# Rotary tables at double width, a gate row that starts later, and the low parts of queries, keys and input forms on another engine

## The chip, the cores and the metric

The kernel runs on one core of a Trainium2 chip. The core has TensorE (matrix products, written PE in a profile), VectorE (DVE), ScalarE (ACT), GpSimd (POOL) and SyncE (SP, which here only issues DMAs); each works through a queue of its own in order, and semaphores tie them together. The metric is the device time of one execution in microseconds, lower is better. Before the change it is 2218.59 us, the median of three runs (2226.13, 2218.59, 2211.78).

## The reference

Two layers of a decoder trunk on a sequence of 1024 with 1024 features, then an RMSNorm. Each layer has four mLSTM heads and four retention heads of width 256 side by side. Cut to what matters:

```python
for l in range(DEPTH):
    shift, scale, gate = split(silu(c) @ w_ada[l] + b_ada[l], 3)
    h = rmsnorm(x, norm_g[l]) * (1 + scale) + shift
    mq, mk, mv, mo, mz, mi, mf, rq, rk, rv, rz = split_cols(h @ w_in[l])
    q, k = split(silu(causal_dwconv([mq, mk], conv_w[l], conv_b[l])), 2)
    y_m = sigmoid(mo) * head_layernorm(mlstm_chunkwise(q, k, mv, mi, mf)) * silu(mz)
    rq, rk = rotary(rq, positions), rotary(rk, positions)
    y_r = head_layernorm(retention_chunkwise(rq, rk, rv)) * silu(rz)
    x = x + gate * ([y_m, y_r] @ w_out[l])
out = rmsnorm(x, final_g)
```

`rotary` rotates the two halves of a head by cos and sin of position times frequency; one table of each, 128 frequencies by 1024 positions, serves both layers and all heads.

## The kernel before

**Products in three parts.** Every float32 operand of a large product is kept as a high part (rounded to a format that TensorE reads at full rate) and a low part (the rest), and a product is three matmuls, high x high, high x low, low x high (`mm3`, L181 to L183). ScalarE makes a high part by a copy; a subtraction makes the low part. For weights that is `high` (L408) and `low` (L413), and the caller chooses the engine of the subtraction: `POOL_LOW` names three of seven weight forms whose low parts are GpSimd's, the rest are VectorE's. For everything else it is `split_to` (L880 to L882): the copy is L881, the subtraction L882, on GpSimd unless another engine is named, and no caller names one. It is called at four places: for the input's forms (`keep` in `build_forms`, 16 pairs in each layer), for queries and keys of every chunk (`split_qk`, 8 heads x 4 chunks x 2 in each layer) and for two rows of the gate in the second layer (`gate_rows`). That makes 162 subtractions of 128x512.

**Strassen-like projections.** The input projection is done by blocks of 2 x 2 with seven products in place of eight. So the input h (kept transposed in `hT`, in two halves of the sequence) is needed in sums and differences of its blocks, U1 to U4, that `build_forms` makes on VectorE (L639 to L660) and splits. The weights are summed likewise, partly by DMAs that add on the way (L714, issued by GpSimd), partly on VectorE (L718). A `Feeder` loads, sums and splits the weights of a product a few slots ahead of it; a slot is the twelve or twenty-four matmuls of one product. Results go to PSUM banks px and pz, and ScalarE and VectorE evacuate them: L780 to L790 for columns, L830 to L840 for values, where L837 adds the bank px to a partial sum and so frees the bank.

**Order.** TensorE's order is written out by hand, slot by slot. Beside the products run generators (`launch`, `tick`): each gets its turn every so many slots and issues its next piece. Such are the forms, the rotary tables, the gate's chain, the adaptive rows, the convolution, and one `attention` per head, that follows a table of 34 steps. The queues of the other engines are ordered by the framework's scheduler; what is issued through `Later` or `late` keeps its program order there.

**Attention.** For every chunk of 256 positions the steps q, k load queries and keys from DRAM, Q, K split them (`split_qk`), S makes scores (L1045 matmuls, L1061 to L1075 on VectorE, split by ScalarE L1083 and GpSimd L1084), V and U use them.

**Rotary tables.** `rotary_tables` (L446, layer 0 only) works in four pieces of 256 positions on half tiles. For each piece it multiplies position by frequency, turns that into a fraction of a full turn in exact parts, and stores the fraction for sine and for cosine, clamped to just below half a turn, to DRAM (`rdr`). `load_rotary` (L977) loads them and applies the sine on ScalarE with a scale of 2 pi.

**Adaptive rows.** `adaptive` (L357) runs beside the products. In layer 0 it makes shift and scale of layer 1 and the gate; in layer 1 it makes the gate by `gate_rows` (L335): for each half eight loads of w_ada of 128x512 and eight multiply-adds (L312, L314), then the split, and two matmuls by ones. Its result is first needed in the output projection at the layer's end.

Of the kernel before, what the change touches and what calls it, by code (L numbers as in the profile page):

```python
# [19 lines left out]
P = 128  # L20
# [67 lines left out]
def tile_hybrid_trunk(ctx, tc, x, xt, c, positions, w_ada, b_ada, norm_g, w_in, w_blk, w_val, conv_w, conv_b,  # L88
# [354 lines left out]

    def rotary_tables():
        V = Later()
        c1, c2, c3 = two_pi_split()  # L446
        ts = [wt("acc", 512, NACC) for _ in range(3)]
        ang, turn, tmp, rnd, a1, pos = (t[:, i * CH:(i + 1) * CH] for t in ts for i in range(2))
        a2 = ang
        for n in range(4):  # L450
            i, cs = n // 2, slice((n % 2) * CH, (n % 2 + 1) * CH)
            if n == 0:
                Q.dma_start(pos.bitcast(I32), positions[0:1, 0:CH].to_broadcast([P, CH]))
                yield 2
            V.tensor_copy(ang, pos.bitcast(I32))
            if n < 3:
                Q.dma_start(pos.bitcast(I32), positions[0:1, (n + 1) * CH:(n + 2) * CH].to_broadcast([P, CH]))
            V.tensor_scalar(ang, ang, kc[:, C_FREQ:C_FREQ + 1], None, ALU.mult)
            V.tensor_copy(a1.bitcast(F32R), ang)
            V.tensor_tensor(a2, ang, a1, ALU.subtract)  # L460
            V.tensor_scalar(turn, a1, c3, None, ALU.mult)
# [3 lines left out]
            for src, cc in ((a1, c2), (a2, c1), (a1, c1)):  # L465
                V.tensor_scalar(tmp, src, cc, None, ALU.mult)
                V.tensor_scalar(rnd, tmp, MAG_I, -MAG_I, ALU.add, ALU.add)
                V.tensor_tensor(tmp, tmp, rnd, ALU.subtract)
                V.tensor_tensor(turn, turn, tmp, ALU.add)
                yield 1  # L470
            parts = ((1, 0.0, tmp), (0, 0.25, a1))
            for which, sh, dst in parts:
                if sh:
                    V.tensor_scalar(turn, turn, sh, None, ALU.add)
                V.tensor_scalar(rnd, turn, MAG_I, -MAG_I, ALU.add, ALU.add)
                V.tensor_tensor(dst, turn, rnd, ALU.subtract)
                yield 1
                V.tensor_scalar(dst, dst, 0.49999994, -0.49999994, ALU.min, ALU.max)
            for which, sh, dst in parts:
                Q.dma_start(rdr[which][i][:, cs], dst)  # L480
# [399 lines left out]
    def split_to(dst, src, eng=G):  # L880
        A.copy(dst[0], src)  # L881
        eng.tensor_tensor(dst[1], src, f(dst[0]), ALU.subtract)  # L882
# [93 lines left out]
    def load_rotary(rot):  # L976
        for which in range(2):  # L977
            for i in range(2):
                t = wt("dm", 512, 2) if which == 0 else wt("nd", 516, 2) if i == 0 else bt()
                Q.dma_start(t[:, 0:HALF], rdr[which][i])  # L980
                A.activation(t[:, 0:HALF], t[:, 0:HALF], AF.Sin, scale=2.0 * math.pi)
# [493 lines left out]
    for l in range(DEPTH):  # L1475
# [147 lines left out]
        launch(adaptive(l, gcol, gb), 2 if l else 30)  # L1623
# [102 lines left out]
```

## Time and profile before

| | |
|---|---|
| median of three runs | 2218.59 us |
| the profiled execution | 2220.83 us |
| its span, first to last instruction | 2219.1 us |
| mean granted TensorE clock | 0.985 |
| HBM read and written | 322.76 and 123.31 MB |

The two layers take about half of the span each. In layer 0 the start-up lasts to about 75 us, the input's forms are built from 76 to 135, the attention of eight heads runs beside the projections from about 280 to 1000, then come the output projection and the norm. Layer 1 repeats that from about 1150; its forms lie at 1170 to 1225. "Busy" of TensorE counts overlapping matmuls once. A group's line in the profile ends with the idle time of the engine just before it, and what ended that idle time; in a list of waits the columns are total us, times, and the longest.

### The profile page before, as it was taken

What the parts mean: (1) busy time and instruction counts of PE and PEld (TensorE: products, weight loads), DVE (VectorE), ACT (ScalarE), POOL (GpSimd) and SP (SyncE); (2) the same over time, 40 slices, a digit from 0 to 9 for tenths busy, and PEclk for the clock granted to TensorE, in tenths of its full rate; (3) what the DMA queues carried; (4) which work ended last, traced back from release to release, by engine and by line L of the source; (5) the groups of instructions that cost most, each with busy time, mean ns of one, the idle gap of its engine ahead of it and who ended that gap; (6) DMA issues with size and microseconds to landing.
All of it is one profiled execution on the core that took longest, in us unless ns stands there. A gap on an engine that the chain in (4) does not pass through costs nothing. (4 is left out here: it accounts for less than half of the span.)

```text
span 2219.1 us, 35050 instructions
## 1 busy us (share of the span) xinstructions
PE 2116.1 (95%) x11489; PEld 1827.4 (82%) x11489; DVE 1785.4 (80%) x3139; ACT 1141.9 (51%) x2151; POOL 949.2 (43%) x820
## 2 busy tenths in 40 slices
PE   7899999999999989999999999999999899999998
PEld 5698889888898878888887788888987887888887
DVE  6898888989989988874639697798897788988563
ACT  7535345445565656553544434444555556555342
POOL 1442345444453454424566344544444354442313
PEclk9999999999999999999999999999999999999999
DMA  8268678787796767686632867868866677687974
GB/s 291 58 189 216 189 218 252 218 241 210 211 249 179 203 188 205 190 270 231 214 105 69 246 198 200 229 184 224 228 189 183 177 214 194 166 211 244 231 251 120
DMA packets 452836, 448.44 MB, mean 202 GB/s; under 512 B 191314, under 2 KB 310042, under 8 KB 452652
## 3 DMA queue, kind: packets, MB, share of 16 engines
q1 hardware_dynamic: 432924, 410.27, 60.4%
q0 software_dynamic: 19584, 35.66, 10.6%
q8 instruction: 90, 1.47, 0.3%
q14 instruction: 94, 0.77, 0.1%
q10 hardware_dynamic: 144, 0.26, 0.0%
HBM read 322.76 MB, written 123.31 MB: 201 GB/s over the span
## 5 line engine op out<-in xcount | busy, mean ns | idle before, releaser
L408 ACT CAST wH<-R 128x512 fp32r<-128x512 f32 x616 | 377.6, 617 | 413.0 <-PE px L182 102.0
L413 POOL TENSOR_TENSOR R<-R,wH 128x512 fp32r<-128x512 f32 x276 | 393.9, 1437 | 457.3 <-ACT wH L408 290.0
L181 PE MATMUL px<-b,wH 128*128 128x512 f32 x912 | 361.1, 396 | 7.6 <-ACT acc L780 5.4
L182 PE MATMUL px<-b,wH 128*128 128x512 f32 x912 | 359.7, 394 | 0.0
L183 PE MATMUL px<-b,R 128*128 128x512 f32 x912 | 359.1, 394 | 0.0
L413 DVE TENSOR_TENSOR R<-R,wH 128x512 fp32r<-128x512 f32 x340 | 263.5, 778 | 98.7 <-ACT wH L408 93.4
L182 PE MATMUL pz<-b,wH 128*128 128x512 f32 x704 | 275.5, 391 | 1.6 <-DVE b L1271 1.6
L181 PE MATMUL pz<-b,wH 128*128 128x512 f32 x704 | 276.0, 392 | 0.0
L183 PE MATMUL pz<-b,R 128*128 128x512 f32 x704 | 275.1, 391 | 0.0
L181 PEld LDWEIGHTS px<-b,wH 128*128 128x128 f32 x912 | 173.5, 190 | 43.9 <-ACT acc L780 6.9
L183 PEld LDWEIGHTS px<-b,R 128*128 128x128 f32 x912 | 173.6, 190 | 37.5
L181 PE MATMUL px<-wH,b 128*128 128x256 f32 (+1 forms) x576 | 176.4, 306 | 26.8 <-DVE acc L837 12.6
L182 PEld LDWEIGHTS px<-b,wH 128*128 128x128 f32 x912 | 173.6, 190 | 33.2
L182 PE MATMUL px<-R,b 128*128 128x256 f32 (+1 forms) x576 | 175.5, 305 | 8.3 <-DVE R L413 8.3
L183 PE MATMUL px<-wH,b 128*128 128x256 f32 (+1 forms) x576 | 174.7, 303 | 0.0
L714 POOL DMA_DIRECT2D R<-in_w_blk_dram x104 | 92.8, 892 | 186.3 <-DMA R<-in_w_blk_dram 85.0
L183 PEld LDWEIGHTS pz<-b,R 128*128 128x128 f32 x704 | 132.6, 188 | 28.4
L182 PEld LDWEIGHTS pz<-b,wH 128*128 128x128 f32 x704 | 132.5, 188 | 27.5 <-DVE b L1271 2.3
L181 PEld LDWEIGHTS pz<-b,wH 128*128 128x128 f32 x704 | 132.7, 188 | 25.7 <-issue 0.2
L181 PEld LDWEIGHTS px<-wH,b 128*128 128x128 f32 x576 | 115.5, 201 | 31.5 <-issue 13.1
L181 PE MATMUL pz<-wH,b 128*128 128x256 f32 (+1 forms) x448 | 134.7, 301 | 1.3 <-DVE acc L790 1.2
L882 POOL TENSOR_TENSOR kc<-acc,kc 128x512 fp32r<-128x512 f32 x64 | 87.4, 1366 | 109.7 <-ACT kc L881 91.6
(343 smaller groups left out, 5327.0 us busy)
## 6 DMA issues: line engine op xcount, KB each, us to landing
R<-in_w_blk_dram SPq DMA_DIRECT2D x276, 256.0 KB
vdr<-acc SPq DMA_DIRECT2D x128, 256.0 KB
ring<-vdr SPq DMA_DIRECT2D x64, 512.0 KB
R<-in_w_out_dram SPq DMA_DIRECT2D x128, 256.0 KB
R<-in_w_blk_dram POOLq DMA_DIRECT2D x104, 256.0 KB, 4.5
R<-in_w_val_dram SPq DMA_DIRECT2D x80, 256.0 KB
gdr<-acc SPq DMA_DIRECT2D x64, 256.0 KB
acc<-in_w_ada_dram SPq DMA_DIRECT2D x64, 256.0 KB
```

The source lines that it names most:

```text
L181: PE.matmul(o, lt[0], rt[0], start=start, stop=False, skip_group_check=more)
L182: PE.matmul(o, lt[0], rt[1], start=False, stop=False, skip_group_check=more)
L183: PE.matmul(o, lt[1], rt[0], start=False, stop=stop, skip_group_check=more)
L408: A.copy(h, r)
L413: eng.tensor_tensor(lo, r, f(h), ALU.subtract)
L714: G.dma_start(raw[n], src, accum_op=ALU.add)
L882: eng.tensor_tensor(dst[1], src, f(dst[0]), ALU.subtract)
```

## The change

Four things are changed:

- `split_to` subtracts on VectorE unless told otherwise. All 162 low parts of L882 leave GpSimd's queue.
- `rotary_tables` works in two pieces of 512 positions, with three tiles of its own kind and three from the pool `big`; it yields at other places, and no longer clamps the fraction. Its rows become half as many and twice as wide, 48 in place of 104; its loads of positions go from four to two, its stores from eight to four.
- The sine's scale is 6.283185, a little below 2 pi, in place of the clamp.
- The adaptive rows of layer 1 start 40 slots after the projections begin, in place of 2.

```diff
--- before.py
+++ after.py
@@ -441,23 +441,25 @@
 
     rdr = [[dpool.tile([P, HALF], F32, name=f"rdr{i}{j}") for i in range(2)] for j in range(2)]
 
+    SIN_SCALE = 6.283185
+
     def rotary_tables():
         V = Later()
         c1, c2, c3 = two_pi_split()
-        ts = [wt("acc", 512, NACC) for _ in range(3)]
-        ang, turn, tmp, rnd, a1, pos = (t[:, i * CH:(i + 1) * CH] for t in ts for i in range(2))
+        ang, tmp, a1 = (wt("acc", 512, NACC) for _ in range(3))
+        turn, rnd, pos = (bt() for _ in range(3))
         a2 = ang
-        for n in range(4):
-            i, cs = n // 2, slice((n % 2) * CH, (n % 2 + 1) * CH)
-            if n == 0:
-                Q.dma_start(pos.bitcast(I32), positions[0:1, 0:CH].to_broadcast([P, CH]))
-                yield 2
+        Q.dma_start(pos.bitcast(I32), positions[0:1, 0:HALF].to_broadcast([P, HALF]))
+        yield 2
+        for i in range(2):
             V.tensor_copy(ang, pos.bitcast(I32))
-            if n < 3:
-                Q.dma_start(pos.bitcast(I32), positions[0:1, (n + 1) * CH:(n + 2) * CH].to_broadcast([P, CH]))
+            if i == 0:
+                Q.dma_start(pos.bitcast(I32), positions[0:1, HALF:T].to_broadcast([P, HALF]))
+            yield 1
             V.tensor_scalar(ang, ang, kc[:, C_FREQ:C_FREQ + 1], None, ALU.mult)
             V.tensor_copy(a1.bitcast(F32R), ang)
             V.tensor_tensor(a2, ang, a1, ALU.subtract)
+            yield 1
             V.tensor_scalar(turn, a1, c3, None, ALU.mult)
             V.scalar_tensor_tensor(turn, a2, c3, turn, ALU.mult, ALU.add)
             V.scalar_tensor_tensor(turn, a2, c2, turn, ALU.mult, ALU.add)
@@ -465,19 +467,17 @@
             for src, cc in ((a1, c2), (a2, c1), (a1, c1)):
                 V.tensor_scalar(tmp, src, cc, None, ALU.mult)
                 V.tensor_scalar(rnd, tmp, MAG_I, -MAG_I, ALU.add, ALU.add)
+                yield 1
                 V.tensor_tensor(tmp, tmp, rnd, ALU.subtract)
                 V.tensor_tensor(turn, turn, tmp, ALU.add)
                 yield 1
-            parts = ((1, 0.0, tmp), (0, 0.25, a1))
-            for which, sh, dst in parts:
+            for which, sh, dst in ((1, 0.0, tmp), (0, 0.25, a1)):
                 if sh:
                     V.tensor_scalar(turn, turn, sh, None, ALU.add)
                 V.tensor_scalar(rnd, turn, MAG_I, -MAG_I, ALU.add, ALU.add)
                 V.tensor_tensor(dst, turn, rnd, ALU.subtract)
-                yield 1
-                V.tensor_scalar(dst, dst, 0.49999994, -0.49999994, ALU.min, ALU.max)
-            for which, sh, dst in parts:
-                Q.dma_start(rdr[which][i][:, cs], dst)
+                yield 2
+                Q.dma_start(rdr[which][i], dst)
             yield 1
 
     def gate_raw(l):
@@ -877,7 +877,7 @@
                 launch(o_gate(got[1, half], g[half], store[half], -1.0, 1 - o))
         return done
 
-    def split_to(dst, src, eng=G):
+    def split_to(dst, src, eng=V):
         A.copy(dst[0], src)
         eng.tensor_tensor(dst[1], src, f(dst[0]), ALU.subtract)
 
@@ -978,7 +978,7 @@
             for i in range(2):
                 t = wt("dm", 512, 2) if which == 0 else wt("nd", 516, 2) if i == 0 else bt()
                 Q.dma_start(t[:, 0:HALF], rdr[which][i])
-                A.activation(t[:, 0:HALF], t[:, 0:HALF], AF.Sin, scale=2.0 * math.pi)
+                A.activation(t[:, 0:HALF], t[:, 0:HALF], AF.Sin, scale=SIN_SCALE)
                 rot[which].append(t[:, 0:HALF])
 
     busy = [False]
@@ -1620,7 +1620,7 @@
 
         slots = slot_order([what for what, _ in jobs])
         feed = Feeder(-1, [job_forms(j) for j in jobs], slots)
-        launch(adaptive(l, gcol, gb), 2 if l else 30)
+        launch(adaptive(l, gcol, gb), 40 if l else 30)
 
         def job_product(what, arg):
             h = arg[0]
```

What becomes of the order. The first place is VectorE's queue in layer 0, where the forms are built (b are the forms' tiles, acc the sums) and where the first weight that TensorE waits for, R_1337, is subtracted. Before:

```order
L651 SCALAR_TENSOR_TENSOR acc_1206<-acc_1199,acc_1203 128x512
L639 TENSOR_TENSOR acc_1243<-b_774,b_775 128x512
L639 TENSOR_TENSOR acc_1245<-b_806,b_807 128x512
L639 TENSOR_TENSOR acc_1247<-b_997,b_998 128x512
L654 TENSOR_TENSOR acc_1203<-acc_1203,acc_1201 128x512
L613 SCALAR_TENSOR_TENSOR acc_1036<-acc_1239,acc_1036 128x512
L649 TENSOR_TENSOR acc_1243<-acc_1243,acc_1245 128x512
L651 SCALAR_TENSOR_TENSOR acc_1250<-acc_1243,acc_1247 128x512
L654 TENSOR_TENSOR acc_1247<-acc_1247,acc_1245 128x512
L413 TENSOR_TENSOR R_1337<-R_1310,wH_1335 128x512
L718 TENSOR_TENSOR R_1310<-R_1310,R_1318 128x512
L613 SCALAR_TENSOR_TENSOR acc_1048<-acc_1300,acc_1048 128x512
```

And now, from the same sum on:

```order
L651 SCALAR_TENSOR_TENSOR acc_1206<-acc_1199,acc_1203 128x512
L639 TENSOR_TENSOR acc_1243<-b_774,b_775 128x512
L639 TENSOR_TENSOR acc_1245<-b_806,b_807 128x512
L639 TENSOR_TENSOR acc_1247<-b_997,b_998 128x512
L613 SCALAR_TENSOR_TENSOR acc_1036<-acc_1239,acc_1036 128x512
L654 TENSOR_TENSOR acc_1203<-acc_1203,acc_1201 128x512
L882 TENSOR_TENSOR b_1209<-acc_1206,b_1208 128x512
L649 TENSOR_TENSOR acc_1243<-acc_1243,acc_1245 128x512
L882 TENSOR_TENSOR b_1213<-acc_1199,b_1212 128x512
L413 TENSOR_TENSOR R_1337<-R_1310,wH_1335 128x512
L882 TENSOR_TENSOR b_1218<-acc_1203,b_1217 128x512
L651 SCALAR_TENSOR_TENSOR acc_1250<-acc_1243,acc_1247 128x512
```

Of the twelve rows before, none was a low part of a form; GpSimd had those. Now two stand between the sums ahead of R_1337 (six more stand further up, eight in all), and two of the sums that were ahead of R_1337 are behind it.

The second place is VectorE's queue some 30 rows on, up to the first L837, which adds the px bank of TensorE's third form of values to a sum; the rows L148 are those of the rotary tables. Before:

```order
L148 TENSOR_SCALAR acc_1444<-acc_1446 128x256
L148 TENSOR_SCALAR acc_1445<-acc_1446 128x256
L148 SCALAR_TENSOR_TENSOR acc_1444<-acc_1444 128x256
L148 TENSOR_SCALAR acc_1445<-acc_1445 128x256
L148 SCALAR_TENSOR_TENSOR acc_1444<-acc_1444 128x256
L148 TENSOR_TENSOR acc_1445<-acc_1445 128x256
L148 TENSOR_TENSOR acc_1444<-acc_1444,acc_1445 128x256
L148 TENSOR_SCALAR acc_1445<-acc_1444 128x256
L413 TENSOR_TENSOR R_1745<-R_1304,wH_1743 128x512
L148 TENSOR_SCALAR acc_1445<-acc_1445 128x256
L148 TENSOR_TENSOR acc_1445<-acc_1445 128x256
L837 TENSOR_TENSOR acc_1619<-px_1402,acc_1619 128x512
```

And now:

```order
L148 CAST acc_1444<-b_1449 128x512
L807 TENSOR_TENSOR acc_1480<-acc_1476,acc_1479 128x512
L639 TENSOR_TENSOR acc_1568<-b_1252,b_1253 128x512
L639 TENSOR_TENSOR acc_1570<-b_970,b_971 128x512
L413 TENSOR_TENSOR R_1736<-R_1304,wH_1734 128x512
L660 SCALAR_TENSOR_TENSOR acc_1570<-acc_1568,acc_1570 128x512
L882 TENSOR_TENSOR b_1574<-acc_1570,b_1573 128x512
L148 TENSOR_SCALAR acc_1444<-acc_1444,kc 128x512
L148 CAST acc_1446<-acc_1444 128x512
L148 TENSOR_TENSOR acc_1444<-acc_1444,acc_1446 128x512
L148 TENSOR_SCALAR b_1447<-acc_1446 128x512
L837 TENSOR_TENSOR acc_1615<-px_1402,acc_1615 128x512
```

In all, fourteen rotary rows of width 256 stood ahead of this first L837, and now five of width 512; four low parts of L882 have come in ahead of it since the sums of the last forms (one is seen here, three stand just ahead).

The third place is VectorE's queue in the attention of layer 0, around the evacuation of a px bank by L837 (kc and q are keys and queries, cf and cL the state). Before:

```order
L413 TENSOR_TENSOR R_4301<-R_3539,wH_4299 128x512
L837 TENSOR_TENSOR acc_4117<-px_3891,acc_4117 128x512
L1104 SCALAR_TENSOR_TENSOR cf_3573<-cf_3573,pa_4234 128x256
L1104 SCALAR_TENSOR_TENSOR cf_3573<-cf_3573,pa_4239 128x256
L1168 BN_STATS st_854_4282<-nd_4060 128x6
```

And now:

```order
L413 TENSOR_TENSOR R_4242<-R_3480,wH_4240 128x512
L882 TENSOR_TENSOR kc_4236<-acc_4080,kc_4236 128x512
L837 TENSOR_TENSOR acc_4058<-px_3832,acc_4058 128x512
L1104 SCALAR_TENSOR_TENSOR cf_3514<-cf_3514,pa_4175 128x256
L882 TENSOR_TENSOR q_4233<-acc_4078,q_4233 128x512
L1104 SCALAR_TENSOR_TENSOR cf_3514<-cf_3514,pa_4180 128x256
L1168 BN_STATS st_857_4223<-nd_4001 128x6
L1169 BN_AGGR mv_4224<-st_857_4223 128x2
```

The low parts of a key and a query now stand ahead of the bank's evacuation and between the two updates of the state.

## The prediction

> **What bounds the kernel now.** The page first, then the stages, then who waits in them.
>
> ```profile
> span 2219.1 us, 35050 instructions
> ...
> PE 2116.1 (95%) x11489; PEld 1827.4 (82%) x11489; DVE 1785.4 (80%) x3139; ACT 1141.9 (51%) x2151; POOL 949.2 (43%) x820
> ```
>
> TensorE sets the time: it is idle in 103 us of 2219.1, so no edit elsewhere can win more than that and what a low clock costs. VectorE comes next, and the change gives it more to do. Whether it has room is read by stage; the table of windows (each column busy us and count, PEclk the granted clock) has the two stages in which the forms of the input are built, 95:145 and 1160:1250, and the four in which attention runs beside the projections:
>
> ```profile
> 95.00:145.00 50.00, 39.18 (x297) 38.80 (x296) 48.01 (x72) 21.43 (x39) 27.36 (x19) 0.90 0.46 129
> 300.00:650.00 350.00, 338.04 (x2064) 303.03 (x2063) 314.93 (x554) 173.78 (x345) 161.16 (x139) 0.99 0.81 228
> 650.00:1000.00 350.00, 337.69 (x1705) 286.35 (x1704) 306.68 (x596) 211.57 (x410) 151.57 (x145) 0.99 0.73 207
> 1160.00:1250.00 90.00, 81.93 (x509) 70.38 (x508) 76.41 (x96) 41.01 (x71) 46.05 (x32) 0.96 0.54 150
> 1330.00:1660.00 330.00, 321.25 (x1972) 289.30 (x1972) 281.29 (x487) 164.82 (x327) 152.48 (x134) 0.99 0.76 209
> 1660.00:2010.00 350.00, 330.46 (x1790) 286.56 (x1789) 286.62 (x549) 201.56 (x397) 159.36 (x156) 0.98 0.70 189
> ```
>
> In 95:145 VectorE is full (48.01 of 50) and TensorE is not (39.18 of 50, clock 0.90). In the attention windows VectorE is idle in 35.1 + 43.3 + 48.7 + 63.4 = 190.5 of 1380 us, TensorE in 52.6. The waits of TensorE, first in the window 95:150, then in 1160:1250, then over the whole span, show what comes late:
>
> ```profile
> PE px L182 <- DVE R L413: 5.6, 1, 5.6
> PE px L181 <- DVE acc L837: 5.2, 1, 5.2
> ...
> PE px L181 <- DVE acc L837: 5.3, 1, 5.3
> PE px L182 <- DVE R L413: 2.7, 2, 2.3
> ...
> PE pa L1126 <- POOL sL L1084: 10.8, 8, 3.4
> ```
>
> Why VectorE is late in the form stage stands in the timelines of VectorE and GpSimd around the first wait (start, length):
>
> ```profile
> 102.01 4.65 DVE L413 TENSOR_TENSOR R<-R,wH 128x512 fp32r<-128x512 f32 x1
> ...
> 98.10 3.44 POOL L882 TENSOR_TENSOR b<-acc,b 128x512 fp32r<-128x512 f32 x2
> 102.10 4.01 POOL L882 TENSOR_TENSOR b<-acc,b 128x512 fp32r<-128x512 f32 x3
> ```
>
> A subtraction took 4.65 us on VectorE while GpSimd did three of exactly the rows that the change moves. The groups of the window 84:107, and over the whole span, say that this is no accident (count, then busy us and mean ns):
>
> ```profile
> L639 DVE TENSOR_TENSOR acc<-b,b 128x512 f32<-128x512 f32 x6 | 8.1, 1404 | 0.0
> L654 DVE TENSOR_TENSOR acc<-acc,acc 128x512 f32<-128x512 f32 x3 | 4.1, 1371 | 0.0
> L651 DVE SCALAR_TENSOR_TENSOR acc<-acc,acc 128x512 f32<-128x512 f32 x3 | 3.0, 990 | 0.1
> L649 DVE TENSOR_TENSOR acc<-acc,acc 128x512 f32<-128x512 f32 x2 | 2.5, 1237 | 0.0
> ...
> L413 DVE TENSOR_TENSOR R<-R,wH 128x512 fp32r<-128x512 f32 x340 | 263.5, 778 | 98.7 <-ACT wH L408 93.4
> L894 DVE SCALAR_TENSOR_TENSOR acc<-acc,cols,acc 128x512 f32<-128x512 f32 x96 | 91.5, 954 | 0.0
> L894 DVE SCALAR_TENSOR_TENSOR acc<-pz,cols,acc 128x511 f32<-128x511 f32 (+2 forms) x48 | 35.5, 739 | 2.3 <-ACT acc L889 1.8
> L1545 DVE TENSOR_TENSOR b<-acc,b 128x512 fp32r<-128x512 f32 x16 | 11.0, 688 | 5.8 <-ACT acc L1541 5.1 <-ACT b L1535 0.7
> ```
>
> L1545 is the same subtraction, in the start-up: 688 ns. L894 takes 739 ns with one operand in PSUM and 954 with both in SBUF. So two-operand SBUF work of VectorE and GpSimd's subtractions block each other.
>
> **The change part by part.** The profiled execution took 2220.83 us (span 2219.1 and 1.7 around it), 2.2 above the median of 2218.59; I make the sum on 2220.83 and take 2 off at the end.
>
> *The low parts.* These rows leave GpSimd (162 in all):
>
> ```profile
> L882 POOL TENSOR_TENSOR q<-acc,q 128x512 fp32r<-128x512 f32 x64 | 94.0, 1468 | 73.8 <-ACT q L881 67.3 <-DMA acc<-kfr 4.2 <-PE pa L183 1.3
> L882 POOL TENSOR_TENSOR kc<-acc,kc 128x512 fp32r<-128x512 f32 x64 | 87.4, 1366 | 109.7 <-ACT kc L881 91.6 <-PE pa L1135 5.4 <-DMA acc<-qdr 4.6
> L882 POOL TENSOR_TENSOR b<-acc,b 128x512 fp32r<-128x512 f32 x32 | 54.1, 1727 | 24.1 <-ACT b L881 24.1
> L413 POOL TENSOR_TENSOR R<-R,wH 128x512 fp32r<-128x512 f32 x276 | 393.9, 1437 | 457.3 <-ACT wH L408 290.0 <-issue 65.7 <-DMA b<-xdr 26.6
> ```
>
> GpSimd loses 94.0 + 87.4 + 54.1 = 235.5 us and two rows of the gate. VectorE gains 162 x 0.688 = 111 us, at the 778 of its L413 126 us. It gets back what those rows made it wait. An upper bound is one block each: 162 x 0.6 = 97 us. A lower one is their share of GpSimd's listed subtractions, 235.5 of 629.4 (37%), in the excess of two listed groups, 340 x 0.09 + 96 x 0.215 = 51 us: 19 us. VectorE's net is thus between +14 and +107 us over the span; I take +50, since the two groups are only a fifth of its busy time.
>
> *Form stage of layer 0.* The five VectorE groups above exceed 0.688 each by 6 x 0.72 + 3 x 0.68 + 3 x 0.30 + 2 x 0.55 and, for the 4.65, 3.97: 12.3 us. In the order 8 low parts now stand ahead of R_1337, costing 8 x 0.688 = 5.5 us. The weight is ready about 7 us sooner, and the 5.6 us wait is gone: -5.6. The Trainium skill ("SBUF — State Buffer", section "SBUF: two separate sides") says that of the two engines the one that starts first holds a shared port pair for its whole instruction while the other is blocked. Read as one turn of waiting, an estimate by it gives R_1337 0.69 + 4.01/3 = 2.0 us, an excess of 9.6, a weight that is 4.1 us sooner and a sum that is 1.5 smaller; the row of 4.65 differs from that, three turns were lost, and the row decides. Late next is L837, which frees the px bank: there the rotary rows help too.
>
> ```profile
> L148 DVE TENSOR_SCALAR acc<-acc 128x256 f32<-128x256 f32 x48 | 17.9, 385 | 0.6
> L148 DVE TENSOR_TENSOR acc<-acc,acc 128x256 f32<-128x256 f32 x24 | 13.2, 552 | 0.5
> L294 DVE TENSOR_SCALAR b<-b,cact 128x512 f32<-128x512 f32 x4 | 1.9, 485 | 0.8 <-DMA b<-in_w_ada_dram 0.8
> ```
>
> By the order 14 rotary rows stood ahead of the first L837, and 5 of double width do now: 14 x 0.47 (between 385 and 552) = 6.6 us against 5 x 0.59 (between 485 and 688) = 2.9. Four low parts now stand there, +2.8 us, while on GpSimd four are gone: they blocked between 0 and 4 x 0.72 (1404 less 688), 2.9. Net 1 to 4 us sooner; I take -3.5 of the 5.2. The window's clock of 0.90 is 50 x 0.10 = 5 us lost after these two gaps; most returns: -4. Sum -13.1.
>
> *Form stage of layer 1.* The same without rotary: 2.7 and 5.3 us of waits, and 90 x 0.04 = 3.6 us of clock. The gate rows of this layer now start 38 slots later, so that this work is out of the stage:
>
> ```profile
> L314 DVE SCALAR_TENSOR_TENSOR acc<-acc,cact,acc 128x512 f32<-128x512 f32 x56 | 58.2, 1040 | 10.8 <-DMA acc<-in_w_ada_dram 10.8
> ```
>
> 14 of the 56 belong to it (two halves of seven), 14.6 us of VectorE. They land in 1330:1660, where VectorE has 48.7 us idle, so they cost nothing there as long as that lasts; if that cover goes they cost up to 14.6. Their 16 loads go behind the stage's weight loads on SyncE's queue, from a DMA share of 0.54 to one of 0.76: not full, 0. For the stage I take -2.7, -4 and -2.5: -9.2, between 0 and -11.6.
>
> *The rest of the rotary tables.* In all 104 rows become 48. By the rates above 104 x 0.47 = 49 us become 48 x 0.59 = 28: VectorE gains 21 us, but behind L837 no wait of TensorE in the rows above stands beside it: -1. The positions and table DMAs (4 and 8) become 2 and 4 on SyncE's queue, without a wait that the rows show: 0. The new scale of the sine and the missing clamp change no count on ScalarE: 0. The three wide buffers come from the big pool; in the order they are taken among the forms' buffers with no extra wait of VectorE or TensorE: 0, and a few us if their first DMA had to wait.
>
> *Score splits.* L1084 keeps its place on GpSimd, which is relieved of 235.5 us. Its eight waits make 10.8 us, and with the clock lost in the four windows (0.01, 0.01, 0.01 and 0.02 of them, 17 us) they bound the gain: between 0 and -28. I take half of the 10.8: -5.
>
> *Attention.* Of the moved rows 123 lie in its four windows (GpSimd's busy us and count at L882):
>
> ```profile
> 300.00:650.00 350.00, 44.74 (x32) 0.99 0.81 228
> 650.00:1000.00 350.00, 39.35 (x28) 0.99 0.73 207
> 1330.00:1660.00 330.00, 43.68 (x32) 0.99 0.76 209
> 1660.00:2010.00 350.00, 43.33 (x31) 0.98 0.70 189
> ```
>
> That is 123 x 0.688 = 85 us more for VectorE, less 14 (123/162 of the 19 above) to 74 (123 x 0.6) back. Of 190.5 us idle, 120 to 180 stay. VectorE's waits become a little longer for whoever stands behind: TensorE's waits for it in these windows are small beside the 190.5, and I charge between 0 and 15: +6.
>
> Sum: -13.1 - 9.2 - 1 - 5 + 6 = -22.3, so 2198.5 on the profiled run and 2196 on the median, 1.0% down.
>
> **The rivals.**
>
> *Given back (no change).* The blocking goes over to the L413 rows, 276 of 1437 ns, that stay on GpSimd and now meet the 162 rows on VectorE. VectorE's net is the upper +107, attention charges the +15, and forms and score splits win 15 instead of 27.3: 2219. For it: L413 is the larger blocker by its 393.9 us. Against: at the 4.65 us row the blocker is L882 alone. The Trainium skill ("Perfetto Trace Analysis", section "Optimizing Scalar/DVE Operations") has this case as a rule: GpSimd and VectorE share a read port, so moving work from one to the other might not help, and it is a saturated VectorE that is to be relieved. By that rule the time stays; the trace bears it out as far as the two do block each other.
>
> *Slower.* The low parts wait for ScalarE's high parts, and these for loads. On GpSimd that was 91.6 + 67.3 = 159 us of waiting in which little stood behind. On VectorE the evacuations of the px and pz banks stand behind (the order shows one right behind a low part many times), and ScalarE and TensorE wait for those. If half of the 159 reaches TensorE, +80 less the 27.3 of forms and score splits: 2219 + 53 = 2272. It cancels the gain from 27 us on and makes 1% slower from 50, a third of the 159. For it: VectorE is at 90% in 300:650, and already waits 93.4 us for L408. Against: with those 93.4 in its queue TensorE was idle for only 52.6 us in all four windows, from all causes; and a queue that is late doesn't wait.
>
> *More.* All waits listed above and their clock return and nothing is charged: 5.6 + 5.2 + 5.3 + 2.7 + 10.8 + 5 + 3.6 and half of attention's 17, in all 47: 2172.
>
> **How the numbers follow.** Within 1% is 2196 to 2241; the three runs of before span 0.65%, so that less than 1% can't be told from none. The forecast, with a range of its own of 2182 to 2210, has 0.42, of which 0.30 lies below 2196 and 0.12 above; more 0.12; given back 0.22; slower 0.24, taken as above 2241. Faster 0.42, same 0.34, slower 0.24. The range reaches from 2172, the end of more, to 2252, into the slower case up to where two fifths of the 159 us come through (61 - 27 = 34 above 2219).
>
> **What would show it.** Right: in 95:145 the clock is near 1.0, no L413 row of VectorE above 2 us, TensorE's waits for L413 and L837 below 2 us each; L639 and L654 near 0.7; GpSimd near 710 us busy; VectorE at 1765 to 1860. Wrong: VectorE rows at L882 with waits on ScalarE above 60 us, TensorE waits for L783, L787, L790 or L894 that grow by tens of us, or new waits for loads, which I have taken as unmoved.

## The result, and the profile after

Four runs of the changed kernel had a median of 2190.99 us (2180.25 to 2195.48), four of the kernel before on the same chip 2222.36 (2211.78 to 2231.77): a ratio of 0.9867, 95% interval 0.9835 to 0.9898. The change makes the kernel 1.3% faster. The forecast was 2196 us. The profiled execution took 2195.48.

The page of the changed kernel, its span and the busy time of each engine:

```profile
span 2193.8 us, 34928 instructions
...
PE 2108.6 (96%) x11489; PEld 1822.2 (83%) x11489; DVE 1757.3 (80%) x3245; ACT 1147.7 (52%) x2151; POOL 726.1 (33%) x658
```

TensorE's idle time went from 103.0 us to 85.2, and its busy time from 2116.1 to 2108.6, at a mean granted clock of 0.987 in place of 0.985. GpSimd lost 223 us. VectorE got 162 subtractions, and is 28 us *less* busy than before. The table of windows of the changed kernel (as in the prediction: PE, PEld, DVE, ACT, POOL, then granted clock, DMA share, GB/s) says in which stages TensorE gained:

```profile
95.00:145.00 50.00, 46.49 (x365) 46.28 (x364) 47.02 (x77) 21.38 (x38) 16.68 (x11) 0.93 0.64 176
145.00:300.00 155.00, 153.63 (x848) 133.15 (x848) 129.56 (x217) 72.44 (x125) 50.23 (x41) 1.00 0.77 220
300.00:650.00 350.00, 336.58 (x2058) 301.66 (x2056) 311.73 (x577) 177.25 (x347) 119.56 (x108) 0.99 0.81 225
650.00:1000.00 350.00, 337.17 (x1689) 286.48 (x1689) 303.30 (x608) 208.00 (x399) 119.03 (x119) 0.99 0.75 213
1160.00:1250.00 90.00, 90.00 (x558) 79.58 (x556) 67.38 (x112) 47.47 (x80) 29.38 (x21) 1.00 0.57 157
1330.00:1660.00 330.00, 318.90 (x1903) 284.69 (x1903) 279.00 (x525) 174.19 (x341) 112.31 (x103) 0.98 0.78 218
1660.00:2010.00 350.00, 335.99 (x1845) 292.58 (x1844) 297.31 (x593) 205.49 (x399) 115.48 (x120) 0.98 0.70 193
```

In the form stages TensorE is busy 46.49 of 50 us in place of 39.18, and all 90 us in place of 81.93 (layer 1's stage begins some 13 us earlier in the changed kernel, so the second pair is not quite the same work; the stretches further down are cut by matmul number and are). In the four attention windows its idle time is 13.4 + 12.8 + 11.1 + 14.0 = 51.3 us, against 52.6.

The waits of TensorE in 95:150, the only row there (the window 1160:1250 has none left), and two rows over the whole span:

```profile
PE px L181 <- DVE acc L837: 3.5, 1, 3.5
```

```profile
PE pa L1126 <- POOL sL L1084: 14.1, 8, 3.2
...
PE pa L183 <- DVE b L934: 2.1, 5, 0.7
```

The timeline of VectorE in the changed kernel around the place where R_1337 is subtracted (start, length), and behind it GpSimd's next subtraction:

```profile
96.00 0.68 DVE L649 TENSOR_TENSOR acc<-acc,acc 128x512 f32<-128x512 f32 x1
96.60 0.68 DVE L882 TENSOR_TENSOR b<-acc,b 128x512 fp32r<-128x512 f32 x1
97.20 0.68 DVE L413 TENSOR_TENSOR R<-R,wH 128x512 fp32r<-128x512 f32 x1
97.80 0.68 DVE L882 TENSOR_TENSOR b<-acc,b 128x512 fp32r<-128x512 f32 x1
98.40 0.68 DVE L651 SCALAR_TENSOR_TENSOR acc<-acc,acc 128x512 f32<-128x512 f32 x1
```

```profile
101.61 4.06 POOL L413 TENSOR_TENSOR R<-R,wH 128x512 fp32r<-128x512 f32 x1 [5.96 <-ACT wH L408]
```

The row that had taken 4.65 us takes 0.68, and the weight is ready at 97.88 in place of 106.66. Every row here goes at one length, low parts included. The groups of the whole span, VectorE's first, then GpSimd's (count, busy us and mean ns, then idle time before them):

```profile
L413 DVE TENSOR_TENSOR R<-R,wH 128x512 fp32r<-128x512 f32 x340 | 247.0, 730 | 89.1 <-ACT wH L408 85.5 <-POOL b L1324 1.5 <-issue 1.3
L894 DVE SCALAR_TENSOR_TENSOR acc<-acc,cols,acc 128x512 f32<-128x512 f32 x96 | 80.4, 838 | 0.0
...
L882 DVE TENSOR_TENSOR q<-acc,q 128x512 fp32r<-128x512 f32 x64 | 47.1, 736 | 15.2 <-ACT q L881 15.2
...
L882 DVE TENSOR_TENSOR kc<-acc,kc 128x512 fp32r<-128x512 f32 x64 | 46.7, 730 | 38.4 <-ACT kc L881 38.4
...
L882 DVE TENSOR_TENSOR b<-acc,b 128x512 fp32r<-128x512 f32 x32 | 22.8, 718 | 3.2 <-ACT b L881 3.2
```

```profile
L413 POOL TENSOR_TENSOR R<-R,wH 128x512 fp32r<-128x512 f32 x276 | 403.8, 1471 | 639.4 <-ACT wH L408 413.5 <-issue 123.7 <-DMA b<-xdr 27.8
...
L1084 POOL TENSOR_TENSOR sL<-acc,sH 128x384 fp32r<-128x384 f32 (+1 forms) x64 | 69.8, 1091 | 127.3 <-ACT sH L1083 101.4 <-issue 7.7 <-DVE cf L1104 6.4
```

The low parts cost VectorE 47.1 + 46.7 + 22.8 = 116.6 us; its L894 fell from 954 to 838 ns and its L413 from 778 to 730. On GpSimd the same three groups had taken 235.5 us.

### The profile page after: what moved, and what is told of

Its sections match the earlier page's. It is cut to its first block, busy times and chain, and to the rows that moved or that the text cites. A ratio compares the mean times of both kernels' runs of the same rounds, so it can differ in the third digit from the quotient of the medians.

```text
span 2193.8 us, 34928 instructions
## 1 busy us (share of the span) xinstructions
PE 2108.6 (96%) x11489; PEld 1822.2 (83%) x11489; DVE 1757.3 (80%) x3245; ACT 1147.7 (52%) x2151; POOL 726.1 (33%) x658
## 3 DMA queue, kind: packets, MB, share of 16 engines
q0 software_dynamic: 19584, 35.66, 10.8%
## 4 chain that ended last, share of the span: by engine, by line
PE 60%; DVE 21%; DMA 9%; issue 6%; ACT 2%; SPq 1%; POOL 1%; DVEq 0%; POOLq 0%; ACTq 0%
PE px L181 8%; PE px L182 8%; PE px L183 8%; PE pz L181 6%; PE pz L182 6%; PE pz L183 6%; PE pa L183 4%; PE pa L182 4%; PE pa L181 4%; DVE acc L894 3%; DVE R L413 2%; PE pa L1135 2%; DMA acc<-qdr 2%; PE pa L1045 1%; DVE R L718 1%
## 5 line engine op out<-in xcount | busy, mean ns | idle before, releaser
L413 POOL TENSOR_TENSOR R<-R,wH 128x512 fp32r<-128x512 f32 x276 | 403.8, 1471 | 639.4 <-ACT wH L408 413.5
L413 DVE TENSOR_TENSOR R<-R,wH 128x512 fp32r<-128x512 f32 x340 | 247.0, 730 | 89.1 <-ACT wH L408 85.5
L181 PE MATMUL px<-wH,b 128*128 128x256 f32 (+1 forms) x576 | 173.8, 302 | 14.7 <-DVE acc L894 4.9
L183 PE MATMUL px<-wH,b 128*128 128x256 f32 (+1 forms) x576 | 172.6, 300 | 0.0
L181 PE MATMUL pz<-wH,b 128*128 128x256 f32 (+1 forms) x448 | 133.9, 299 | 0.0
L183 PE MATMUL pz<-wH,b 128*128 128x256 f32 (+1 forms) x448 | 133.7, 298 | 0.0
L182 PE MATMUL pz<-R,b 128*128 128x256 f32 (+1 forms) x448 | 133.6, 298 | 0.0
```

What stands on the lines that cost most here:

```text
L181: PE.matmul(o, lt[0], rt[0], start=start, stop=False, skip_group_check=more)
L182: PE.matmul(o, lt[0], rt[1], start=False, stop=False, skip_group_check=more)
L183: PE.matmul(o, lt[1], rt[0], start=False, stop=stop, skip_group_check=more)
L413: eng.tensor_tensor(lo, r, f(h), ALU.subtract)
```

## The experiments

Theory A: VectorE's subtractions of two SBUF operands and GpSimd's block each other, and the gain is the blocks that are gone. Theory B: the gain comes from the rotary rows and the later gate. Theory C: it comes from GpSimd's shorter queue, whose weight and score rows no longer stand behind low parts. Each ratio is against the kernel before on the same chip.

### The parts of the change

**Rotary and gate alone.** The changed kernel with the low parts back on GpSimd:

```diff
-    def split_to(dst, src, eng=V):
+    def split_to(dst, src, eng=G):
```

> The rotary and gate row changes alone; all 162 low parts of L882 back on GpSimd. Theory A (GpSimd's subtractions block VectorE, above all while the forms are built): most of the gain goes, 2207 to 2218 us, and in the stages of the forms TensorE waits for L413 and L837 for 4 to 10 us again. Theory B (the rotary and gate row changes make the gain, the low parts are neutral): 2188 to 2195. Theory C (the gain is GpSimd's shorter queue, 235 us less work, whatever its rows block): 2210 to 2220.

Measured: 2220.54 us median of 12, ratio 1.0017 (0.9998 to 1.0036), just above the ranges of A and C and far from B's. These edits bring nothing by themselves, and theory B falls; the gate, the rotary rows and the sine's scale were not tried apart. Its waits of TensorE in 95:145 are again those of before:

```profile
PE px L182 <- DVE R L413: 5.6, 1, 5.6
PE px L181 <- DVE acc L837: 5.3, 1, 5.3
```

**Low parts alone.** The kernel before with the one default changed:

```diff
-    def split_to(dst, src, eng=G):
+    def split_to(dst, src, eng=V):
```

> The kernel before with only the default of split_to changed, so the low parts alone. A: 2195 to 2205, the wait of TensorE for L413 gone from the stage of the forms in layer 0. B: 2217 to 2226. C: 2195 to 2205, without a word on which wait goes.

Measured: 2190.46 us, ratio 0.9887 (0.986 to 0.9914) against 0.9835 to 0.9898 for the whole change. That is a larger gain than A and C gave it (2195 to 2205). One word carries it. Its page says what that word does to VectorE, with rotary rows as they were:

```profile
PE 2101.0 (96%) x11489; PEld 1815.4 (83%) x11489; DVE 1764.4 (81%) x3301; ACT 1146.4 (52%) x2151; POOL 723.7 (33%) x658
```

VectorE did 162 rows more than before and was busy for less.

**Forms alone.** The changed kernel, default back to GpSimd, `keep` names VectorE:

```diff
-            split_to(pair, t)
+            split_to(pair, t, V)
...
-    def split_to(dst, src, eng=V):
+    def split_to(dst, src, eng=G):
```

> The changed kernel, but only the forms' 32 low parts on VectorE; queries, keys and gate rows (130) back on GpSimd. A: 2190 to 2199, nearly all the gain, since the waits that went are in the stages of the forms. B: 2188 to 2195. C: the 32 rows are 54 of the 243 us, so a fifth of the low parts' gain: about 2207 to 2214.

Measured: 2200.86 us, ratio 0.9943 (0.9922 to 0.9964): between A's range, which gave the forms nearly all of the gain, and C's, which gave them a fifth. The form stages are as in the changed kernel: R_1337's wait is gone in layer 0, and no wait is left in layer 1's.

**Queries and keys alone.** The same with `split_qk` in place of `keep`:

```diff
-                split_to((t[:, 0:512], t[:, 512:1024]), raw)
+                split_to((t[:, 0:512], t[:, 512:1024]), raw, V)
...
-    def split_to(dst, src, eng=V):
+    def split_to(dst, src, eng=G):
```

> The changed kernel, but only the low parts of queries and keys (128) on VectorE; forms and gate rows (34) back on GpSimd. A: 2203 to 2215, with TensorE's waits for L413 and L837 of 4 us or more back in the stages of the forms. B: 2188 to 2195. C: 181 of the 243 us are off GpSimd, three quarters of the low parts' gain: 2194 to 2202.

Measured: 2204.34 us, ratio 0.995 (0.9935 to 0.9966), in A's range and slower than C's. The form stages keep the waits of before (5.6, 5.3, 5.2 and 2.7 us), so this part wins elsewhere. Forms and queries with keys bring about half each, a division that neither theory had.

### Is it the block, or the length of GpSimd's queue?

Two kernels give GpSimd more work again next to each query's and key's split, whose low parts had taken 181.4 us of it (94.0 + 87.4). In the first it is spent on subtractions that read SBUF, in the second almost wholly on fills that read nothing; nobody reads what this work writes. Theory D, in the expectations, is a further rival: a low part is ready sooner because VectorE needs less time for it.

```diff
                 split_to((t[:, 0:512], t[:, 512:1024]), raw)
+                if not spare:
+                    spare.append(wt("rows", P, 2))
+                s = spare[0]
+                for c in (0, P, 2 * P):
+                    G.tensor_tensor(s, raw[:, c:c + P], f(t[:, c:c + P]), ALU.subtract)
```

> The changed kernel, and after each of the 128 splits of a query or key GpSimd repeats three quarters of the subtraction (three of 128x128) into a tile that nothing reads. The result is unchanged. Theory A (what GpSimd reads in SBUF blocks VectorE): the attention's part of the gain goes, 2198 to 2210, since VectorE keeps its rows and is blocked again. Theory C (GpSimd's queue was too long): 2198 to 2206 as well, but then the kernel with idle fills below rises as much. Theory D (the low part is ready sooner because VectorE needs 0.73 us for it and GpSimd 1.3): 2188 to 2195, no change.

```diff
                 split_to((t[:, 0:512], t[:, 512:1024]), raw)
+                if not spare:
+                    spare.append(wt("rows", P, 2))
+                s = spare[0]
+                G.tensor_tensor(s[:, 0:2], raw[:, 0:2], f(t[:, 0:2]), ALU.subtract)
+                for _ in range(5):
+                    G.memset(s, 0.0)
```

> As the one before, but GpSimd's idle work is a subtraction of 128x2, which waits for the same copy, and five fills of 128x128 that read nothing: its queue is as long as with three subtractions, and it reads nothing of SBUF. A: 2188 to 2196, as without the idle work, and VectorE's rows keep their durations. C: 2198 to 2206. D: 2188 to 2195.

Measured: with the subtractions 2233.79 us, ratio 1.008 (1.0056 to 1.0104); with the fills 2200.17, ratio 0.9921 (0.9897 to 0.9944). The engines' busy time and three groups, first with the subtractions:

```profile
PE 2123.5 (95%) x11489; PEld 1828.1 (82%) x11489; DVE 1815.3 (81%) x3245; ACT 1145.6 (51%) x2151; POOL 977.4 (44%) x1042
```

```profile
L894 DVE SCALAR_TENSOR_TENSOR acc<-acc,cols,acc 128x512 f32<-128x512 f32 x96 | 82.1, 856 | 0.0
L1115 DVE TENSOR_TENSOR cL<-cf,cH 128x512 fp32r<-128x512 f32 (+1 forms) x80 | 66.3, 829 | 3.7 <-ACT cH L1113 3.6
L882 DVE TENSOR_TENSOR q<-acc,q 128x512 fp32r<-128x512 f32 x64 | 52.5, 820 | 15.9 <-ACT q L881 15.9
```

and with the fills (L1115 above and L1116 here are the L1109 of the changed kernel):

```profile
PE 2107.8 (96%) x11489; PEld 1819.3 (83%) x11489; DVE 1755.1 (80%) x3245; ACT 1147.5 (52%) x2151; POOL 912.2 (41%) x1426
```

```profile
L894 DVE SCALAR_TENSOR_TENSOR acc<-acc,cols,acc 128x512 f32<-128x512 f32 x96 | 78.7, 820 | 0.0
L1116 DVE TENSOR_TENSOR cL<-cf,cH 128x512 fp32r<-128x512 f32 (+1 forms) x80 | 58.2, 728 | 4.6 <-ACT cH L1114 4.6
...
L882 DVE TENSOR_TENSOR q<-acc,q 128x512 fp32r<-128x512 f32 x64 | 44.0, 688 | 16.3 <-ACT q L881 16.3
```

186 us of work that is mostly fills (912.2 - 726.1) left VectorE's busy time as it was (1755.1 against 1757.3). 251 us of subtractions (977.4 - 726.1) added 58 us to it, in rows like those of cL (829 ns against 728 with the fills), of q (820 against 688) and of L894 (856 against 820), and the kernel took 33.6 us longer than that with the fills. The two loads are not equally long, 251 against 186 us, but in the windows 145:300, 300:1000 and 1250:2010 TensorE waits for GpSimd as long in both (21.1 us with the subtractions, 20.7 with the fills), and for VectorE 32.7 us against 18.6. So the block is the larger cost, as theory A has it, though no theory had a time as long as 2233.79 (A's range ended at 2210). Theory D, which foresaw no change in either kernel, falls. But a longer queue is not free: the fills' time lies in C's range (2198 to 2206) and not in A's (2188 to 2196). Their ratio is 0.5 to 0.6% above those of the changed kernel (0.9867, and 0.9859 below), so some 12 to 14 us, about two fifths of the gain, may belong to theory C (the fills' interval begins at 0.9897, where the change's first ends, 0.9898). It shows in part in the score rows (L1084 of the changed kernel), for which TensorE waits 20.7 us in the attention windows, against 15.9 and 12.7 in the changed kernel's two profiles. The Trainium skill ("SBUF — State Buffer", section "SBUF: two separate sides") makes the same distinction: a VectorE instruction with two SBUF inputs contends only with a GpSimd instruction that reads SBUF. These two runs agree.

### Would more of it be better?

**Score splits on VectorE too**, and **the weight forms of the projections too** (204 of GpSimd's 276 weight rows; 72 of other products stay there):

```diff
-            G.tensor_tensor(lo, src, f(hi), ALU.subtract)
+            V.tensor_tensor(lo, src, f(hi), ALU.subtract)
```

> The changed kernel with the low part of the scores (L1084, 64 rows) on VectorE too. A: 64 rows of 0.5 to 0.6 us more on VectorE, 21 us of blocks less; TensorE's waits for L1084 (15.9 us beside 14.1 of one kind) shrink to a few, since GpSimd's 1.1 us row and the work ahead of it in its queue go: 2176 to 2188. Rival (VectorE's queue is what a score's low part would then wait in): 2190 to 2200, with TensorE waiting for L1084 on VectorE as long as it did on GpSimd.

```diff
-    POOL_LOW = ("S1", "S3", "a22")
+    POOL_LOW = ()
```

> The changed kernel with the weight forms' low parts that GpSimd still has in the projections (those named in POOL_LOW) on VectorE too. A carried on: about 190 us of rows come to VectorE, 134 us of blocks by L413 go, so VectorE is busier by 40 to 60 us and TensorE's waits hardly move: 2183 to 2196. Rival (VectorE becomes the bound, since weights come late behind evacuations): 2205 to 2240, with TensorE's waits for L413 on VectorE above 20 us.

Measured: 2197.6 us, ratio 0.9922 (0.9895 to 0.9949), with the score splits, and 2202.45, ratio 0.9944 (0.9923 to 0.9965), with the weights. Theory A had foreseen 2176 to 2188 and 2183 to 2196, and missed both; the first time lies in its rival's range, the second below its rival's. Neither is better than the change, and the second is worse. The waits of TensorE that name L934 (the convolution's sums, on VectorE), and VectorE's weight rows, in the kernel with the score splits (first fence) and in that with the weights (second and third):

```profile
PE pa L183 <- DVE b L934: 13.4, 7, 5.4
...
PE pa L1126 <- DVE sL L1084: 5.5, 6, 1.4
```

```profile
PE pa L183 <- DVE b L934: 18.4, 6, 7.2
```

```profile
L413 DVE TENSOR_TENSOR R<-R,wH 128x512 fp32r<-128x512 f32 x544 | 374.4, 692 | 112.1 <-ACT wH L408 109.7 <-POOL b L1324 1.5
```

With these weight forms gone from GpSimd the weight rows of VectorE run almost unblocked (692 ns), and its busy time hardly grows (1760.1 us with 204 rows more). Yet TensorE now waits 18.4 us for L934, which was 2.1 in the changed kernel, and 13.4 in the other of the two. The subtractions that stand in VectorE's queue wait 109.7 us for ScalarE's high parts, 85.5 in the changed kernel, and what is behind them waits too; that L934 is late for this reason was not tried by itself. The score splits did what was hoped on their own place, 5.5 us of waits in place of 14.1, so that their rival's reason (a score's low part would wait as long in VectorE's queue) is not what was seen; what was won there was lost at L934.

### The same kernels again, stage by stage

TensorE does 11489 matmuls in every kernel. Their starts cut an execution into four stretches: up to number 2000 (start-up, forms of layer 0), 2000 to 6000 (attention and output of layer 0), 6000 to 7000 (forms of layer 1), and 7000 to the last. To see how far two profiles of one kernel agree there, four were taken again, unchanged:

> A second profile of the kernel before, to read how far two profiles of one kernel differ stage by stage. The yardstick is the start of the k-th matmul of 11489 (TensorE's count does not change): in the first profile number 2000 started at 375.3 us, 6000 at 1170.0, 7000 at 1358.8, the last at 2211.2. Theory F (stages are repeatable): each of the four stretches between these places agrees within 2 us with the first profile. Theory N (only the form stages are repeatable): the two form stretches (to 2000, and 6000 to 7000) agree within 2 us, an attention stretch (2000 to 6000, 7000 to the end) differs by 4 to 10 us.

> The low parts of the forms alone on VectorE again. In its first profile it led the kernel before by 18.4 us at matmul 2000, gained another 11.1 in layer 1's form stage, and lost 15 us again in the two attention stretches. Theory G (the gain of the forms is really given back in attention while queries and keys stay on GpSimd): attention loses at least 8 us again. Theory N (that loss was the scatter of one profile): it loses less than 5 us against the mean of the two profiles of before. The ratio stays 0.992 to 0.996 by both, since it was timed already.

> The low parts of queries and keys alone on VectorE again. In its first profile the two attention stretches were 13 us shorter than before's and the form stages did not change but for 7 us by matmul 2000. Theory A (fewer GpSimd subtractions that block VectorE shorten attention): 5 us or more shorter than the mean of before's two profiles again. Theory N: between 5 shorter and 5 longer. The ratio stays 0.993 to 0.997.

> The changed kernel again, timed beside the parts. If the two parts add up (theory A) its ratio is 0.986 to 0.991; if the parts partly cancel or help one another, outside that. By matmul 2000 it leads the kernel before by 16 to 20 us, in layer 1's form stage it gains another 10 to 12, and in the two attention stretches it is between 6 us shorter and 6 longer than the mean of before's profiles.

Measured: before again, one run, 2212.13 us; forms again 0.994 (0.9921 to 0.996); queries and keys again 0.9968 (0.9948 to 0.9988); the change again 2186.32 us, ratio 0.9859 (0.9826 to 0.9892). The stretches, worked out from the starts in each trace, and beside them the sum of TensorE's waits in the windows 145:300, 300:1000 and 1250:2010:

```
us                       to 2000  2000-6000  6000-7000  7000-last  waits
before                     375.3      794.7      188.7      852.4   56.8
before again               372.1      796.6      188.1      845.7   54.9
rotary and gate alone      368.7      791.7      190.9      850.3   55.1
forms                      356.9      797.2      182.7      859.9   62.0
forms again                356.6      803.7      182.5      853.0   62.2
queries, keys              367.8      796.5      184.6      840.9   44.4
queries, keys again        367.4      797.0      187.3      843.4   46.0
low parts alone            360.5      797.5      179.1      841.4   55.2
the change                 357.0      800.1      177.3      851.1   54.8
the change again           353.4      797.5      177.3      843.2   46.3
idle subtractions          358.9      822.2      179.1      863.7   76.8
idle fills                 357.7      802.4      175.8      855.2   60.2
score splits too           356.2      803.5      177.8      849.3   54.9
weight forms too           356.6      805.1      175.2      857.9   61.2
```

Two profiles of one kernel agree within 4 us in the form stages (before's first stretch differs by 3.2, more than the 2 that theory N allowed) and within 8 in attention (before's last stretch by 6.7). So theory F falls, and one profile can't tell 8 us in attention. TensorE's waits scatter as much: 54.8 and 46.3 us in the change's two profiles. Against the mean of before's two profiles:

- The change takes 18.5 us off up to 2000 and 11.1 off in 6000 to 7000 (means of its two profiles); attention is 3.2 longer in layer 0 and 1.9 shorter in layer 1. In its second profile it leads before's first by 21.9 us at 2000, where 16 to 20 were expected, and its second ratio is a hair below the expected 0.986.
- Forms alone win 17.0 and 5.8 us and lose 4.8 and 7.4 in attention, 12.0 together in the second profile, which is what theory G asked for: a part of what the forms win is given back later while queries and keys stay on GpSimd. (The same sum differs by 10.5 us between the change's two profiles, so the size is uncertain.) TensorE's waits rise to 62 us there. Why, no run settles.
- Queries and keys alone take 10 us off the waits in the last column (44.4 and 46.0 in place of 54.9 to 56.8). What falls are waits for VectorE (23.5 and 22.8 before, 15.6 and 17.1 now) and for ScalarE (21.0 and 21.3, now 13.3 twice); those for GpSimd, whose queue is shorter, rise (12.3 and 10.8, now 15.5 and 15.6). That speaks against theory C for this part. Their attention stretches together were 5.8 us shorter in the mean, but 4.3 in the second profile, which is short of the 5 of theory A; what carries this part is the two ratios, and the waits point the same way.
- By the ratios the parts make 0.58% and 0.41% (means of two), 1.0% together, against 1.1% for the low parts alone and 1.3 and 1.4 for the whole. Each part was tried in the changed kernel, so the nearer base is rotary and gate alone (1.0017): from there they make 0.76% and 0.58%, 1.3% together, against 1.5 and 1.6 for the whole. Within the intervals the parts add up. Whether rotary and gate help a little once the low parts have moved stays open.

## Why the prediction came out right, and where its steps did not

The time came out near the forecast, 2196 against 2190.99 and 2186.32, and by the mechanism that carried it: subtractions on GpSimd had been holding up VectorE. The gain was 1.3 and 1.4% where 1.0 was forecast, and several terms were wrong. Step by step:

**The blocks, and the late weight.** Right but for one sign. R_1337's row fell from 4.65 to 0.68 us, it was ready 8.8 us sooner (7 were expected), and its wait is gone in every kernel with the forms on VectorE and back in every one without. None of VectorE's L413 rows in that stage is above 2 us, and L654 is at 682 ns over the whole span (1202 before). L639, which was to be near 0.7 us, is not: over the whole span its mean fell from 1153 to 829 ns, but in 95:145 it is 1155, where it was 1142. What blocks it there now are GpSimd's weight rows, as the last section shows.

**Layer 0's form stage, -13.1 and -1 for rotary, and layer 1's, -9.2.** Right in kind and short in size: 18.5 and 11.1 us were measured. Part of what I missed lies in a window that I had not looked at, the one behind the stage, of which this was the row before the change:

```profile
145.00:300.00 155.00, 151.02 (x844) 132.15 (x843) 129.03 (x235) 67.11 (x114) 50.27 (x42) 0.98 0.74 210
```

TensorE was idle for 4.0 us there at a clock of 0.98, and is now for 1.4 at 1.00. This part goes with the rotary rows: TensorE's waits in that window are 3.1 to 5.8 us in the three profiles with the old rows (two of before, low parts alone) and 0 to 1.9 in all with the new. In 95:145 the clock was to return to near 1.0; it was 0.90 and 0.86 in before's two profiles and is 0.93 and 1.00 in the change's, so by one profile the sign failed and by the other it held.

**L837, -3.5 of 5.2.** The step that failed in its cause, and in size: 1.7 us went, and it stays above the 2 us that were the sign. I put it down to rotary rows that no longer stand ahead. With rotary and gate alone the wait is still 5.3 us, and so it is with queries and keys moved too; with the forms moved it is 3.3; with all low parts alone, rotary rows as they were, 2.2; with everything 3.5. What shortens it is the forms' low parts that leave GpSimd. The new rotary rows do shorten the stretch up to 2000 by 5 us (368.7 against 373.7), but behind that stage, in the window just named, and by the ratio of 1.0017 nothing of it shows in the whole time.

**VectorE's net, +50 between +14 and +107.** Wrong, in its upper bound on what comes back. It took one block for each row, 162 x 0.6 = 97 us, though the quoted row of 4.65 us had lost three turns. With low parts alone VectorE took 162 rows of about 0.73 us, 118, and went from 1781.7 (mean of two profiles of before) to 1764.4: 135 us came back, beyond the bound. Each row on GpSimd had cost VectorE more (135/162 = 0.83 us) than VectorE now spends on it. With that VectorE, at 1757 us, ended below the 1765 to 1860 that were a sign of being right. GpSimd was to be at 710 us and is at 726.1; 9.9 us of that are its 276 weight rows, which became 34 ns longer each.

**Attention, +6.** Wrong as a charge for queries and keys: with them alone TensorE's waits fell by 10 us, those for VectorE's L934 among them (4.2 and 5.9 us in the two profiles of before, 2.8 and 2.7 with queries and keys moved). In the whole change this and the forms' losses cancel: +3.2 and -1.9 us.

**Score splits, -5.** Wrong. GpSimd lost 223 us, and TensorE's waits for L1084 over the whole span went from 10.8 to 14.1 us (10.7 in the second profile of the change). By the fills' kernel a longer queue makes these waits longer, so a shorter one should have helped, and something else came in between. The rows wait 101.4 us for ScalarE's sH on GpSimd, where it was 41.9; whether that is what holds them up, or only an emptier queue that reaches them sooner, stays open. The -5 and the +6 together made +1, and attention was 3.2 - 1.9 = +1.3: two errors cancelled, and that the attention came out as forecast was luck.

**The rivals.** *Given back* was wrong: the 276 weight rows that stay on GpSimd do meet the moved ones (1437 ns became 1471), but a block costs less than what the low parts had cost. The Trainium skill's rule ("Perfetto Trace Analysis", section "Optimizing Scalar/DVE Operations"), that moving work between the two might not help, did not hold for the low parts: 1.3% faster, with VectorE less busy. For the weight forms it did by the outcome, 0.9944 in place of 0.9867, though not by its reason: VectorE's weight rows ran at 692 ns there. *Slower* had a real mechanism with its dose too large: the moved rows wait 38.4 + 15.2 + 3.2 = 56.8 us on VectorE for ScalarE, 53.6 of them for queries and keys, where it was 159 on GpSimd, which fits a fuller queue that reaches them later. (Two fifths of the 159 are 64 us, so the range's upper end by its own reckoning was 2255 and not 2252; nothing hangs on it.) With the score splits or the weights moved as well TensorE does wait longer for VectorE, at L934. *More* needed all the waits to go; L837's 3.5 us and the score rows' 14.1 are still there.

## What to carry to other kernels

Before moving elementwise work off GpSimd to a busy VectorE, compare VectorE's own rows: where those with both operands in SBUF are longer in one stage than elsewhere (here 13 to 104%), see in the timeline whether GpSimd's subtractions lie beside them; if so, the move can leave VectorE less busy. Move first what stands ahead of a wait of TensorE (here 32 of 162 rows gave about half of the gain), and stop when the gain turns into new waits for VectorE.

A stage sum from one profile is good to a few us where a stage repeats; for the rest of the kernel take a second profile before reading a difference of less than 8 us.

## What the hardware showed

Either of the two engines can lose several turns in a row. Before, VectorE's row of 4.65 us lost three to GpSimd. Now GpSimd's row at 101.61, shown above, took 4.06 us while VectorE did this (its timeline in the changed kernel):

```profile
102.02 0.69 DVE L718 TENSOR_TENSOR R<-R,R 128x512 f32<-128x512 f32 x1
102.62 0.68 DVE L882 TENSOR_TENSOR b<-acc,b 128x512 fp32r<-128x512 f32 x1
103.22 0.68 DVE L413 TENSOR_TENSOR R<-R,wH 128x512 fp32r<-128x512 f32 x1
103.82 0.68 DVE L882 TENSOR_TENSOR b<-acc,b 128x512 fp32r<-128x512 f32 x1
104.42 0.68 DVE L831 TENSOR_TENSOR acc<-pz,acc 128x512 f32<-128x512 f32 x1
105.03 2.89 DVE L639 TENSOR_TENSOR acc<-b,b 128x512 f32<-128x512 f32 x2
107.84 0.68 DVE L831 TENSOR_TENSOR acc<-pz,acc 128x512 f32<-128x512 f32 x1
```

Four rows with both operands in SBUF went at full speed. GpSimd's row ended at 105.67, 1.25 us after the start of L831, which has an operand in PSUM; that is near the 4.01/3 = 1.34 us of its rows before. Then the two L639 rows took 2.89 us for 1.36, beside the next two of GpSimd's weight rows (1.63 us from 105.74 on, and 1.75 from 107.33). But the turn doesn't always stay with one engine. From 84.06 us on in the kernel before, GpSimd's rows took 1.73 to 1.82 us and VectorE's three L639 rows beside them 1.72 to 1.79, one turn each, though both engines had their next row ready. What decides between the two patterns is open; no run tested it.

The second surprise is the price of small GpSimd work. The groups of the fills' kernel:

```profile
L1019 POOL MEMSET rows<- 128x128 f32 x640 | 138.2, 216 | 31.9
...
L1017 POOL TENSOR_TENSOR rows<-acc,q 128x2 f32<-128x2 f32 x64 | 33.3, 520 | 78.9 <-ACT q L881 53.6 <-issue 10.8 <-DMA R<-in_w_blk_dram 5.1
```

A subtraction of two columns took 520 ns, one of 128 columns in the other kernel 699 (x192 on queries). So some 520 of the 699 ns don't depend on the number of columns. This may be why 251 us of short ones cost VectorE 58 us, where the 235.5 us of 128x512 rows had cost it 135.
